# Down projections in 1024-column blocks, 9 of 22 pairs of k tiles by seven products, inner features in two sets, weight sums in place

## The chip, the cores and the metric

The kernel runs on one core of one Trainium2 chip. The metric is the device time of one execution in microseconds (us), the median of several runs. All arithmetic is float32. A product of float32 matrices is made from a rounded high part (`hi`, type fp32r) and a remainder (`lo`), as `x_hi*w_hi + x_hi*w_lo + x_lo*w_hi`: three matmuls of 128x128 by 128x512 for one product of a k tile.

## The reference, cut to what matters

Two layers; each is a mixer (retention and a gating unit in layer 0, a linear recurrence and sparse attention in layer 1) and then this feed-forward part, for 256 rows `x` of 2048 columns and 5632 inner features:

```
def swiglu(h, wg, wu, wd):
    return (jax.nn.silu(h @ wg) * (h @ wu)) @ wd
...
        h = rms_norm(x, ln_ffn_g[layer])
        x = x + swiglu(h, w_ffn_gate[layer], w_ffn_up[layer], w_ffn_down[layer]).astype(x.dtype)
```

The weights of the feed-forward parts are 264 of the loads of 1 MB of the kernel. The change touches only the feed-forward parts.

## The kernel before

**Units.** All weights come as loads of 1 MB into `raw` (three buffers), 128 partitions by 2048 numbers. In the feed-forward part a load is one *unit*. `ffn` makes the list of units in the order of the computation and issues each unit's preparation one unit ahead of its use (`AHEAD = 1`). The 5632 inner features are 11 groups of 512. Before, they go in three sets of 4, 4 and 3 groups: gate and up projections of the groups of a set (8 units for each group: a unit is two k tiles of 128 rows, gate and up columns side by side), then the down projection of that set, in four column blocks of 512 (`Down`; a unit is four k tiles).

**Plain units** (`"r"` in `KINDS`, made by `whole`). ScalarE rounds `raw` to `hi` in two halves of 1024 (`piece`, line 107), VectorE subtracts `lo = raw - hi` (line 108). TensorE makes 8 products, 24 matmuls. `hi` and `lo` have four buffers each (`HI`), so that a cast waits until TensorE is through with an earlier half.

**Seven-product units** (`"s"`, units 0, 3 and 6 of each group in `GateUp`). Seven products in the place of eight, 21 matmuls, after Winograd's form of Strassen's scheme: the two row halves of the activations and the four 128x512 blocks of the weights are combined by sums ahead of the products, and the seven results (PSUM banks `q1` to `q8`, without a number) are combined after them. `sums` makes the sums of the weights: three adds on VectorE (lines 300 to 302, 1024, 512 and 512 elements) from `raw` into a tile of their own, `sum`; `hi` and `lo` of the four sums (line 108 again); `hu` and `lu`, the two parts of three blocks as they came (lines 309 and 310, 1536 elements; one buffer each). `left` makes the sums of the activations. After the last seven-product unit of a group, `inner` takes four adds on VectorE out of PSUM; after the last unit of the group `outer` takes four more (line 371), a Silu (line 373) and a multiplication (line 374) for each half.

**Names in the texts.** M0, R1, R2, M3, R4, R5, M6, R7 are the units of a group: M for seven products, R for plain. The *boundary* of a group is R7, then the transposes of the results of an earlier group (`pt_hid`, 8 matmuls; `to_mix2`, put off in the list `late` and done at `flush`), then M0 and R1 of the next group.

**Order.** The order of the instructions on each engine isn't that of the code: a scheduler in the language places them, with the code's order as priority. Each engine works through its own list in that fixed order, and semaphores tie the engines together.

Of the kernel before, what the change touches and what calls it, by code (L numbers as in the profile page):

```python
# [31 lines left out]
KINDS = "srrsrrsr"  # L32
AHEAD = 1
FIRST = (1, 0, 2, 3, 4, 5, 6, 7)
MIXED = tuple(i for i, c in enumerate(KINDS) if c == "s")
# [5 lines left out]
def trunk(ctx: ExitStack, tc: tile.TileContext, d: dict, out: bass.AP):  # L41
# [18 lines left out]

    def T(shape, name, dt=F32):
        return now["T"].tile([128, *shape], dt, tag="T", name=name)
# [10 lines left out]
    def mix_tile(name):  # L73
        return act.tile([128, 2, 2, S], F32R, tag="B", name=name)
# [35 lines left out]

    def whole(src):

        raw = load(src, 2048)
        out = []
        for o in (0, 1024):
            hi, lo = piece(raw, o, 2, 512)
            out += [(hi[:, i, :], lo[:, i, :]) for i in range(2)]
        return out
# [105 lines left out]
    def left(src, gs):  # L224

        g, h = T([4, 128], "g"), T([4, 128], "h")
        nc.scalar.activation(g[:, 0:4:3, :], src[:, 0, :].rearrange("p (i n) -> p i n", i=2), AF.Copy, scale=gs[0])
        nc.scalar.activation(g[:, 1:3, :], src[:, 1, :].rearrange("p (i n) -> p i n", i=2), AF.Copy, scale=gs[1])
        nc.vector.tensor_sub(h[:, 0, :], g[:, 3, :], g[:, 2, :])
        nc.vector.tensor_sub(h[:, 3, :], g[:, 0, :], g[:, 3, :])  # L230
        nc.vector.tensor_sub(h[:, 1, :], h[:, 0, :], g[:, 0, :])
        nc.vector.tensor_add(h[:, 2, :], g[:, 1, :], h[:, 1, :])
        out = []
        for t, n in ((g, 3), (h, 4)):
            a = act.tile([128, 2, 4, 128], F32R, tag="A", name="A", bufs=8 + len(MIXED))
            nc.scalar.copy(a[:, 0, 0:n, :], t[:, 0:n, :])
            nc.vector.tensor_sub(a[:, 1, 0:n, :], t[:, 0:n, :], a[:, 0, 0:n, :].bitcast(F32))
            out += [(a[:, 0, i, :], a[:, 1, i, :]) for i in range(n)]
        return out

    class Norm:
# [8 lines left out]
        def operand(self, i, src):  # L250
            gs = [gain(self.g0 + 2 * i), gain(self.g0 + 2 * i + 1)]
            if i in self.mixed:
                self.tiles.append(left(src, gs))
# [60 lines left out]
    class GateUp:  # L314
# [4 lines left out]
        def __init__(self, n, hid, first):  # L319
            self.n, self.q, self.hid, self.first = n, {}, hid, first  # L320
            self.order = FIRST if first else range(8)

        def product(self, i, x2, hi, lo, last=False):
# [3 lines left out]
            (xh, xl), ps = x2, self.q[i]  # L327
# [4 lines left out]
        def use(self, i, w):  # L332
            j, end = self.order[i], i == 7
            if KINDS[j] != "s":
                a = self.n.tiles[j]
                for e, kt, cols in ((0, 0, ((2, 0), (4, 1))), (1, 1, ((2, 0), (4, 1))), (3, 0, ((3, 0), (8, 1))), (2, 1, ((3, 0), (8, 1)))):
                    for b, th in cols:
                        t = slice(128 * th, 128 * th + 128)
                        self.product(b, (a[:, kt, 0, t], a[:, kt, 1, t]), *w[e], end and e in (1, 2))
            else:  # L340
                a11, a12, a22, d1, d2, d3, d4 = self.n.tiles[j]
                s1, s2, s3, s4, b11, b21, b22 = w
                last = not any(k in MIXED for k in self.order[i + 1 :])
                self.product(5, d1, *s1, last)
                self.product(7, d4, *s2, last)
                self.product(6, d2, *s3, last)
                self.product(4, a22, *s4)
                self.product(1, a11, *b11, last)
                self.product(2, a12, *b21)
                self.product(3, d3, *b22)  # L350
                if last:
                    self.inner()
            if i == (0 if self.first else 7):
                flush()
            if end:
                self.outer()

        def inner(self):
            q = self.q
            c1, u2, u3, v, w = (T([512], n) for n in ("c1", "u2", "u3", "v", "w"))  # L360
            nc.scalar.copy(c1, q[1])
            nc.vector.tensor_add(u2, c1, q[6])
            nc.vector.tensor_add(u3, u2, q[7])
            nc.vector.tensor_sub(v, q[5], u2)
            nc.vector.tensor_sub(w, q[5], u3)
            self.c = {2: c1, 4: u3, 3: v, 8: w}

        def outer(self):
            c, n, s = self.c, self.n, []
            for i in (4, 2, 3, 8):  # L370
                nc.vector.tensor_add(c[i], self.q[i], c[i])
# [4 lines left out]
            late.append(partial(to_mix2, s, "hid", self.hid))  # L376

    class Down:


        def __init__(self, c, hid, total, done):
            self.c, self.hid, self.total, self.done = c, hid, total, done

        def use(self, i, w):
            xs = pairs(self.hid)
            if i == 0:
                self.ps = two(512, "pd")
            end = i == self.total - 1
            order = [(j, th) for th in range(2) for j in range(4)] if end else [(j, th) for j in range(4) for th in range(2)]
            for j, th in order:  # L390
                xh, xl = xs(4 * i + j)
                t = slice(128 * th, 128 * th + 128)
                hi, lo = w[j]
                mm(self.ps[th], xh[:, t], hi, start=i + j == 0, stop=False)  # L394
                mm(self.ps[th], xh[:, t], lo, start=False, stop=False)  # L395
                mm(self.ps[th], xl[:, t], hi, start=False, stop=end and j == 3)  # L396
            if i == 0:
                flush()
            if end:
                add_x(self.c, self.ps)  # L400
                self.done(self.c)

    def ffn(layer, n, norm):
        wgu, wd = d[f"wgu{layer}"], d[f"wd{layer}"]
        f = stage(f"f{layer}", TF)
        fp = f.enter_context(tc.tile_pool(name=f"sums{layer}", bufs=1))

# [8 lines left out]
        for g0, gn in ((0, 4), (4, 4), (8, 3)):  # L416
            hid = []
            for g in range(g0, g0 + gn):
                gu = GateUp(n, hid, g == 0)
                units += [(wgu[g, j], KINDS[j], partial(gu.use, i)) for i, j in enumerate(gu.order)]  # L420
            for c in range(4):
                dn = Down(c, hid, gn, done if g0 == 8 else lambda c: None)
                units += [(wd[c, g0 + i], "r", partial(dn.use, i)) for i in range(gn)]
        ready = {}
        for i, (_, _, use) in enumerate(units):
            for k in range(i, min(i + AHEAD + 1, len(units))):
                src, kind, _ = units[k]
                if k not in ready:
                    ready[k] = sums(src, fp) if kind == "s" else whole(src)
# [14 lines left out]
    lp = c0.enter_context(tc.tile_pool(name="l0", bufs=1))  # L444
    lng = lp.tile([128, 2, 512], F32, name="lng")
# [167 lines left out]
    lp = c1.enter_context(tc.tile_pool(name="l1", bufs=1))  # L613
    masks = lp.tile([128, 7, 128], I32, name="masks")
# [355 lines left out]
def _gate_up(g, u):  # L970

    g, u = (w.reshape(8, 2, 128, -1, 512).transpose(3, 0, 2, 1, 4) for w in (g, u))
    return np.ascontiguousarray(np.stack([g[:, :, :, 0], g[:, :, :, 1], u[:, :, :, 1], u[:, :, :, 0]], 3)).reshape(-1, 8, 128, 2048)
# [33 lines left out]
def _layout(i):  # L1007
# [11 lines left out]
    for l in range(2):  # L1019
        o[f"wgu{l}"] = _gate_up(i["w_ffn_gate"][l], i["w_ffn_up"][l])  # L1020
        o[f"wd{l}"] = _wide(i["w_ffn_down"][l], 512)
# [29 lines left out]
```

## Time and profile before

| | before |
|---|---|
| median of 3 runs | 2218.31 us (2217.01 to 2219.98) |
| the profiled execution: its time | 2217.86 us |
| its span, first to last instruction | 2216.1 us |
| TensorE matmuls (PE) | 10199, busy 2203.8 us |
| TensorE weight loads (PEld) | busy 1830.6 us |
| VectorE (DVE) | busy 1622.4 us |
| ScalarE (ACT) | busy 1121.1 us |
| GpSimd (POOL) | busy 12.1 us |
| mean granted TensorE clock | 1.000 |

Busy times overlap, since the engines work side by side. Matmuls are pipelined and the ends of their records are modelled, so the time that a matmul costs in a full stream is read from the distance of the starts.

### The profile page before, as it was taken

Reading aid. Unit: us, or ns where it says so; the run is one execution under the profiler, and the core shown is the slowest. Engines: PE = TensorE matmul, PEld = TensorE weight load, DVE = VectorE, ACT = ScalarE, POOL = GpSimd, SP = SyncE. Lnnn points to the kernel's source line nnn. Section 1 sums busy time; section 2 is a strip of 40 time slices with the busy share of each in tenths; the row PEclk is TensorE's granted clock in tenths of the full one; section 3 lists DMA queues with packets and bytes.
Section 4 is the critical chain, followed back from the end, with each engine's and each line's share of the span. In section 5 each row is a group of like instructions: output and inputs, shape, how many; then the busy total and the mean of one; then the engine's idle time right before and its main releaser. Section 6 shows DMA issues by size and latency. Waiting matters only on the chain.

```text
span 2216.1 us, 26309 instructions
## 1 busy us (share of the span) xinstructions
PE 2203.8 (99%) x10199; PEld 1830.6 (83%) x10199; DVE 1622.4 (73%) x2227; ACT 1121.1 (51%) x1368; POOL 12.1 (1%) x24
## 2 busy tenths in 40 slices
PE   9999999999999999999999999999999999999999
PEld 7888878888888888888888888888888888888887
DVE  6745657988568975797655788869886688857884
ACT  6444435655445553555555355556554455534543
POOL 0000000000000000000000000000000000000000
PEclk9999999999999999999999999999999999999999
DMA  8555465555555555555455443354555555555554
GB/s 330 199 189 198 156 162 209 190 206 195 186 192 209 190 190 193 205 186 208 165 198 189 148 152 114 133 180 186 209 209 179 207 200 191 191 191 209 188 192 152
DMA packets 63437, 419.67 MB, mean 189 GB/s; under 512 B 7672, under 2 KB 7672, under 8 KB 15696
## 3 DMA queue, kind: packets, MB, share of 16 engines
q1 hardware_dynamic: 60704, 412.51, 51.0%
q0 software_dynamic: 1312, 3.33, 0.8%
q10 hardware_dynamic: 1296, 2.15, 0.3%
q8 instruction: 80, 1.31, 0.2%
q14 instruction: 45, 0.37, 0.0%
HBM read 414.29 MB, written 3.67 MB: 189 GB/s over the span
## 4 chain that ended last, share of the span: by engine, by line
PE 97%; DVE 1%; DMA 1%; ACT 0%; issue 0%; SPq 0%; ACTq 0%
PE q L328 14%; PE q L329 14%; PE q L330 14%; PE pd L396 7%; PE pd L395 7%; PE pd L394 7%; PE po L161 2%; PE po L162 2%; PE po L160 2%; PE pqk L161 1%; PE pqk L162 1%; PE pqk L160 1%; PE plv L818 1%; DMA raw<-in_ev_out 1%; PE pt_hid L201 1%; PE pvs L160 1%
## 5 line engine op out<-in xcount | busy, mean ns | idle before, releaser
L108 DVE TENSOR_TENSOR lo<-raw,hi 128x1024 fp32r<-128x1024 f32 (+3 forms) x652 | 780.2, 1207 | 457.6 <-ACT hi L107 454.5
L107 ACT CAST hi<-raw 128x1024 fp32r<-128x1024 f32 (+3 forms) x652 | 674.5, 1039 | 737.7 <-PE pd L396 216.7
L328 PE MATMUL q<-hi,A 128*128 128x512 f32 x1144 | 446.7, 390 | 0.0
L329 PE MATMUL q<-lo,A 128*128 128x512 f32 x1144 | 446.0, 390 | 0.0
L330 PE MATMUL q<-hi,A 128*128 128x512 f32 x1144 | 445.2, 389 | 0.0
L394 PE MATMUL pd<-hi,hid 128*128 128x512 f32 x704 | 275.2, 391 | 0.0
L396 PE MATMUL pd<-hi,hid 128*128 128x512 f32 x704 | 274.0, 389 | 0.0
L395 PE MATMUL pd<-lo,hid 128*128 128x512 f32 x704 | 274.0, 389 | 0.0
L328 PEld LDWEIGHTS q<-hi,A 128*128 128x128 f32 x1144 | 214.8, 188 | 45.5
L330 PEld LDWEIGHTS q<-hi,A 128*128 128x128 f32 x1144 | 214.8, 188 | 45.3
L329 PEld LDWEIGHTS q<-lo,A 128*128 128x128 f32 x1144 | 214.8, 188 | 44.9
L107 ACT CAST hi<-sum 128x1024 fp32r<-128x1024 f32 x132 | 138.6, 1050 | 189.9 <-PE q L330 81.7
L108 DVE TENSOR_TENSOR lo<-sum,hi 128x1024 fp32r<-128x1024 f32 x132 | 161.6, 1224 | 68.4 <-ACT hi L107 64.7
L396 PEld LDWEIGHTS pd<-hi,hid 128*128 128x128 f32 x704 | 132.1, 188 | 27.5
L395 PEld LDWEIGHTS pd<-lo,hid 128*128 128x128 f32 x704 | 132.2, 188 | 27.0
L394 PEld LDWEIGHTS pd<-hi,hid 128*128 128x128 f32 x704 | 132.2, 188 | 27.0
L309 ACT CAST hu<-raw 128x1536 fp32r<-128x1536 f32 x66 | 97.7, 1480 | 56.9 <-PE q L330 40.0
L310 DVE TENSOR_TENSOR lu<-raw,hu 128x1536 fp32r<-128x1536 f32 x66 | 115.7, 1753 | 3.7 <-ACT hu L309 3.6
L300 DVE TENSOR_TENSOR sum<-raw 128x1024 f32<-128x1024 f32 x66 | 80.6, 1221 | 3.3 <-DMA raw<-in_wgu 2.7
L328 PE MATMUL q<-hu,A 128*128 128x512 f32 x198 | 78.4, 396 | 0.2
L330 PE MATMUL q<-hu,A 128*128 128x512 f32 x198 | 78.4, 396 | 0.0
L329 PE MATMUL q<-lu,A 128*128 128x512 f32 x198 | 77.7, 392 | 0.0
(379 smaller groups left out, 3026.4 us busy)
## 6 DMA issues: line engine op xcount, KB each, us to landing
raw<-in_wgu SPq DMA_DIRECT2D x176, 1024.0 KB, 4.8
raw<-in_wd SPq DMA_DIRECT2D x88, 1024.0 KB, 4.8
raw<-in_ev_in SPq DMA_DIRECT2D x44, 1024.0 KB, 4.8
raw<-in_od_in SPq DMA_DIRECT2D x32, 1024.0 KB, 4.8
raw<-in_ev_out SPq DMA_DIRECT2D x16, 1024.0 KB, 4.8
raw<-in_od_out SPq DMA_DIRECT2D x16, 1024.0 KB, 4.7
raw<-in_od_z SPq DMA_DIRECT2D x8, 720.0 KB, 4.0
raw<-in_ev_in SPq DMA_DIRECT2D x6, 512.0 KB, 7.4
```

Of the source, the lines that this page charges most:

```text
L107: nc.scalar.copy(hi[:, :e], raw[:, o : o + e])
L108: nc.vector.tensor_sub(lo[:, :e], raw[:, o : o + e], hi[:, :e].bitcast(F32))
L160: mm(ps[th], xh[:, c], hi[:, j, :], start=i + j == 0, stop=False)
L300: nc.vector.tensor_add(sm[:, 0:2, :], r[:, 0:3:2, :], r[:, 3:4, :].to_broadcast([128, 2, 512]))
L309: nc.scalar.copy(hu, r[:, 0:3, :])
L310: nc.vector.tensor_sub(lu, r[:, 0:3, :], hu.bitcast(F32))
L328: mm(ps, xh, hi, start=first, stop=False)
L329: mm(ps, xh, lo, start=False, stop=False)
L330: mm(ps, xl, hi, start=False, stop=last)
L394: mm(self.ps[th], xh[:, t], hi, start=i + j == 0, stop=False)
L395: mm(self.ps[th], xh[:, t], lo, start=False, stop=False)
L396: mm(self.ps[th], xl[:, t], hi, start=False, stop=end and j == 3)
```

## The change

It makes a single class `Block` for the gate/up groups and for the down projection. The inner features go in two sets, of 6 and 5 groups. The down projection of a set goes in two column blocks of 1024 (`cp` 0 and 1), 12 or 10 units each; a unit is one pair of k tiles with the four 128x512 blocks of the weights, as in a gate/up unit. Of the pairs 1, 3, 5, 7, 9 (first set) and 1, 3, 5, 7 (second set) the products are seven, in both column blocks. So these pairs' activations `hid` are made by `left` (sums of the row halves), where the others keep `split`. In the second column block each seven-product unit stands ahead of the plain one before it. The results are added to `x` straight from the PSUM banks (`grow`), half of them after the last seven-product unit and half after the last unit.

`right` takes the place of `whole` and `sums`: it makes `hu` and `lu` first, then sums the blocks of weights in place in `raw`, then `hi` and `lo` of the sums. The tile `sum` is gone, and the room goes to 17 buffers for `hid` in the place of 8. The order of the products in a seven-product unit is now 1 (with `hu`), 5, 7, 6 (sums), 2, 3 (`hu`), 4 (a sum) in the code; before it was 5, 7, 6, 4 (sums), then 1, 2, 3 (`hu`).

```diff
-KINDS = "srrsrrsr"
-AHEAD = 1
+SETS = ((0, 6), (6, 5))
+MIXED = (0, 3, 6)
...
+HIDDEN = {6: (1, 3, 5, 7, 9), 5: (1, 3, 5, 7)}
...
-    def sums(src, fp):
+    def right(src, mixed, pool):
...
         raw = load(src, 2048)
-        r = raw.rearrange("p (i n) -> p i n", i=4)
-        sm = fp.tile([128, 4, 512], F32, tag="sum", name="sum")
-        nc.vector.tensor_add(sm[:, 0:2, :], r[:, 0:3:2, :], r[:, 3:4, :].to_broadcast([128, 2, 512]))
-        nc.vector.tensor_add(sm[:, 2, :], sm[:, 0, :], r[:, 2, :])
-        nc.vector.tensor_add(sm[:, 3, :], sm[:, 2, :], r[:, 1, :])
         parts = []
-        for i in range(2):
-            hi, lo = piece(sm.rearrange("p i n -> p (i n)"), 1024 * i, 2, 512)
-            parts += [(hi[:, e, :], lo[:, e, :]) for e in range(2)]
-        hu = fp.tile([128, 3, 512], F32R, tag="hu", name="hu")
-        lu = fp.tile([128, 3, 512], F32R, tag="lu", name="lu")
-        nc.scalar.copy(hu, r[:, 0:3, :])
-        nc.vector.tensor_sub(lu, r[:, 0:3, :], hu.bitcast(F32))
-        parts += [(hu[:, i, :], lu[:, i, :]) for i in range(3)]
+        if mixed:
+            r = raw.rearrange("p (i n) -> p i n", i=4)
+            hu = pool.tile([128, 3, 512], F32R, tag="hu", name="hu")
+            lu = pool.tile([128, 3, 512], F32R, tag="lu", name="lu")
+            nc.scalar.copy(hu, r[:, 0:3, :])
+            nc.vector.tensor_sub(lu, r[:, 0:3, :], hu.bitcast(F32))
+            parts += [(hu[:, i, :], lu[:, i, :]) for i in range(3)]
+            nc.vector.tensor_add(r[:, 0:4:3, :], r[:, 0:3:2, :], r[:, 3:4, :].to_broadcast([128, 2, 512]))
+            nc.vector.tensor_add(r[:, 2, :], r[:, 0, :], r[:, 2, :])
+            nc.vector.tensor_add(r[:, 1, :], r[:, 2, :], r[:, 1, :])
+        for o in (1024, 0):
+            hi, lo = piece(raw, o, 2, 512)
+            parts += [(hi[:, i, :], lo[:, i, :]) for i in range(2)]
         return parts
...
+            if j in self.mixed:
+                a11, a12, a22, d1, d2, d3, d4 = a
+                b11, b21, b22, s3, s2, s1, s4 = w
+                last = not any(k in self.mixed for k in self.order[i + 1 :])
+                self.product(1, a11, b11, last)
+                self.product(5, d1, s1, last)
+                self.product(7, d4, s2, last)
+                self.product(6, d2, s3, last)
+                self.product(2, a12, b21)
+                self.product(3, d3, b22)
+                self.product(4, a22, s4)
+                if last:
+                    self.inner(self.q)
...
+            def keep():
+                for i in range(2):
+                    src = turn([t[:, 256 * i : 256 * i + 256] for t in s], "pt_hid")
+                    if flags[i]:
+                        hid.append(left(src, (1.0, 1.0), lambda: mix_tile("hid").rearrange("p a b (c n) -> p a (b c) n", n=128)))
+                    else:
+                        m = mix_tile("hid")
+                        split(m, src)
+                        hid.append(m)
...
+    def down(w, cp, hid, mixed, n, done):
+        def grow(q):
+            for i, (th, e) in ((2, (0, 0)), (3, (0, 1)), (4, (1, 0)), (8, (1, 1))):
+                xs = x[2 * cp + e][:, th, :]
+                nc.vector.tensor_add(xs, q[i], xs)
...
+        order = list(range(n))
+        if cp:
+            for j in mixed:
+                order[j - 1], order[j] = j, j - 1
+        return Block(w, hid, order, mixed, n - 1 if cp else 0, lambda q: grow(inner_sums(q)), outer).units()
...
-        for g0, gn in ((0, 4), (4, 4), (8, 3)):
+        for g0, gn in SETS:
```

What it does to the lists of the engines is seen best at the boundary of a group. The first place is VectorE's list in layer 0, from the sums of the next group's M0 on. Before (`u`, `v`, `w`, `c` are the partial sums of the finished group, `lo<-sum` belongs to a seven-product unit, `lo<-raw` to a plain one):

```order
L300 TENSOR_TENSOR sum<-raw 128x1024
L301 TENSOR_TENSOR sum<-sum,raw 128x512
L108 TENSOR_TENSOR lo<-raw,hi 128x1024
L302 TENSOR_TENSOR sum<-sum,raw 128x512
L108 TENSOR_TENSOR lo<-raw,hi 128x1024
L108 TENSOR_TENSOR lo<-sum,hi 128x1024 x2
L362 TENSOR_TENSOR u_5504<-c_5503,q_5268 128x512
L363 TENSOR_TENSOR u_5505<-u_5504,q_5264 128x512
L364 TENSOR_TENSOR v<-q_5260,u_5504 128x512
L365 TENSOR_TENSOR w<-q_5260,u_5505 128x512
L310 TENSOR_TENSOR lu<-raw,hu 128x1536
```

And of the change, the same boundary between the inner adds of a group (which stand just ahead of these rows) and the first `lo` of R1 (seven rows stand between these and it); L299 is `lu`, L301 to L303 are the sums, L372 are the outer adds, L202 and L223 to L225 make `hid`:

```order
L299 TENSOR_TENSOR lu<-raw,hu 128x1536
L372 TENSOR_TENSOR v<-q_4418,v 128x512
L301 TENSOR_TENSOR raw<-raw 128x2x512
L372 TENSOR_TENSOR w<-q_4439,w 128x512
L302 TENSOR_TENSOR raw<-raw 128x512
L372 TENSOR_TENSOR c_4639<-q_4414,c_4639 128x512
L303 TENSOR_TENSOR raw<-raw 128x512
L111 TENSOR_TENSOR lo<-raw,hi 128x1024
L202 TENSOR_TENSOR hid<-pt_hid,hid 128x2x256
L111 TENSOR_TENSOR lo<-raw,hi 128x1024
L223 TENSOR_TENSOR h<-g 128x128
L224 TENSOR_TENSOR h<-g 128x128
```

The three sums and the two `lo` of M0 stood ahead of the inner adds and now stand behind them, and `lu` of M0 is ahead of its sums in the place of behind them.

The second place is ScalarE's list at the same boundaries. Before, from the inner copy `c` on (`hu` is M0's, `hi<-raw` are those of R1 and R2):

```order
L361 COPY c_5503<-q_5276 128x512
L309 CAST hu<-raw 128x1536
L107 CAST hi<-raw 128x1024
L373 ACTIVATE u_5505<-u_5505,r 128x512
L207 CAST hid<-pt_hid 128x2x256 x2
L373 ACTIVATE c_5503<-c_5503,r 128x512
L107 CAST hi<-raw 128x1024 x3
```

And of the change (the first two `hi` are M0's, the two in one row are R1's; `g` and `h` are the tiles of `left`, L374 is the Silu):

```order
L359 COPY c_4639<-q_4398 128x512
L298 CAST hu<-raw 128x1536
L110 CAST hi<-raw 128x1024
L201 CAST hid<-pt_hid 128x2x256
L110 CAST hi<-raw 128x1024
L221 ACTIVATE g<-pt_hid 128x2x128
L222 ACTIVATE g<-pt_hid 128x256
L374 ACTIVATE c_4639<-c_4639,r 128x512
L230 CAST hid<-g 128x384
L110 CAST hi<-raw 128x1024 x2
L230 CAST hid<-h 128x512
L374 ACTIVATE u_4641<-u_4641,r 128x512
```

Both `hi` of M0, which before stood ahead of the copy, now stand behind it, and the work of `left` stands between them and the rest.

The third place is TensorE's list at the same boundary of the change, from the end of M0 into R1 (lines 326, 327 and 328 are the three matmuls of a product; `q_4755`, `q_4751`, `q_4776` and `q_4759` are the banks of R1):

```order
L327 MATMUL q_4759<-lo,A 128x512
L328 MATMUL q_4759<-hi,A 128x512
L326 MATMUL q_4755<-hi,A 128x512
L326 MATMUL q_4751<-hi,A 128x512
L326 MATMUL q_4776<-hi,A 128x512
L326 MATMUL q_4759<-hi,A 128x512
L327 MATMUL q_4755<-lo,A 128x512
L328 MATMUL q_4755<-hi,A 128x512
```

In the rows of before every product's three matmuls stand together (`hi`, `lo`, `hi`, as in the down projection):

```order
L394 MATMUL pd_4363<-hi,hid 128x512
L395 MATMUL pd_4363<-lo,hid 128x512
L396 MATMUL pd_4363<-hi,hid 128x512
L394 MATMUL pd_4364<-hi,hid 128x512
L395 MATMUL pd_4364<-lo,hid 128x512
L396 MATMUL pd_4364<-hi,hid 128x512
```

In the change, four matmuls with `hi` of R1 stand ahead of the first that needs its `lo`.

## Rows read from the trace of the kernel before

**Rows 1.** Page, part 1: busy us (share of the span) and instructions.

```profile
PE 2203.8 (99%) x10199; PEld 1830.6 (83%) x10199; DVE 1622.4 (73%) x2227; ACT 1121.1 (51%) x1368; POOL 12.1 (1%) x24
```

**Rows 2.** Waits of PE, the longest: us in total, times, longest us.

```profile
PE po L160 <- ACT hi L107: 2.7, 1, 2.7
```

**Rows 3.** Windows, a group and a down projection: us; PE, PEld, DVE, ACT busy.

```profile
509.27:557.35 48.08, 48.08 (x217) 39.63 (x215) 41.54 (x46) 26.05 (x27) 0.00 (x0) 1.00 0.58 214
558.10:646.20 88.10, 88.10 (x396) 73.04 (x395) 50.20 (x50) 36.56 (x37) 0.00 (x0) 1.00 0.53 191
```

**Rows 4.** Timeline of PE (start us, us), down projection, two starts 24 matmuls apart.

```profile
640.06 0.39 PE L394 MATMUL pd<-hi,hid 128*128 128x512 f32 x1
...
645.50 0.39 PE L394 MATMUL pd<-hi,hid 128*128 128x512 f32 x1
```

**Rows 5.** Timeline of PE at a boundary: starts of M6, R7, transposes, M0, R1.

```profile
504.45 0.39 PE L328 MATMUL q<-hi,A 128*128 128x512 f32 x1
...
509.27 0.39 PE L328 MATMUL q<-hi,A 128*128 128x512 f32 x1
...
514.74 0.27 PE L201 MATMUL pt_hid<-ident,c 128*128 128x128 f32 x1
...
515.53 0.48 PE L328 MATMUL q<-hi,A 128*128 128x512 f32 x1
...
520.44 0.39 PE L328 MATMUL q<-hi,A 128*128 128x512 f32 x1
520.67 0.40 PE L329 MATMUL q<-lo,A 128*128 128x512 f32 x1
```

**Rows 6.** Timeline of DVE at the same boundary.

```profile
504.60 0.68 DVE L302 TENSOR_TENSOR sum<-sum,raw 128x512 f32<-128x512 f32 x1
...
509.64 0.68 DVE L362 TENSOR_TENSOR u<-c,q 128x512 f32<-128x512 f32 x1
...
512.16 1.75 DVE L310 TENSOR_TENSOR lu<-raw,hu 128x1536 fp32r<-128x1536 f32 x1
513.83 0.69 DVE L371 TENSOR_TENSOR u<-q,u 128x512 f32<-128x512 f32 x1
514.43 0.68 DVE L371 TENSOR_TENSOR c<-q,c 128x512 f32<-128x512 f32 x1
...
518.45 0.75 DVE L374 SCALAR_TENSOR_TENSOR u<-w,r,u 128x512 f32<-128x512 f32 x1
519.12 4.63 DVE L108 TENSOR_TENSOR lo<-raw,hi 128x1024 fp32r<-128x1024 f32 x4
```

**Rows 7.** Groups by form, ACT: count, busy us, mean ns, idle before.

```profile
L107 ACT CAST hi<-raw 128x1024 fp32r<-128x1024 f32 x624 | 653.5, 1052 | 713.3 <-PE pd L396 214.2 <-PE q L330 169.4 <-PE po L162 63.9
...
L309 ACT CAST hu<-raw 128x1536 fp32r<-128x1536 f32 x66 | 97.7, 1480 | 56.9 <-PE q L330 40.0 <-DMA raw<-in_wgu 9.6 <-ACT hi L107 7.2
...
L207 ACT CAST hid<-pt_hid 128x512 fp32r<-128x512 f32 x44 | 23.6, 588 | 1.0
...
L373 ACT ACTIVATE c<-c,r 128x512 f32<-128x512 f32 x22 | 16.0, 725 | 0.0
```

**Rows 8.** Tiles of `left` (g, h): ns min/median/max, first and last start.

```profile
L227 ACT ACTIVATE g<-pxt,gains x6: 465/466/470, 358.6 to 1509.1; 128x256 f32<-128x256 f32 x6
...
L236 ACT CAST A<-g x6: 513/514/515, 359.4 to 1510.0; 128x384 fp32r<-128x384 f32 x6
L229 DVE TENSOR_TENSOR h<-g x6: 282/284/289, 359.8 to 1510.4; 128x128 f32<-128x128 f32 x6
...
L237 DVE TENSOR_TENSOR A<-g,A x6: 551/552/555, 360.4 to 1511.0; 128x384 fp32r<-128x384 f32 x6
...
L237 DVE TENSOR_TENSOR A<-h,A x6: 683/692/692, 361.9 to 1514.0; 128x512 fp32r<-128x512 f32 x6
```

**Rows 9.** Timeline of PE soon after the start, two neighbours.

```profile
8.42 0.63 PE L161 MATMUL pvs<-lo,A 128*128 128x512 f32 x1
8.84 0.63 PE L162 MATMUL pvs<-hi,A 128*128 128x512 f32 x1
```

More of the change, by code (lines that the diff above doesn't have):

```diff
@@ new lines, in right, with __init__, units, product @@
+        for o in (1024, 0):
+            hi, lo = piece(raw, o, 2, 512)
+            parts += [(hi[:, i, :], lo[:, i, :]) for i in range(2)]
+        return parts
+    class Block:
+        def __init__(self, w, a, order, mixed, flush_at, inner, outer):
+            self.w, self.a, self.order, self.mixed, self.flush_at, self.inner, self.outer = w, a, order, mixed, flush_at, inner, outer
+            self.q = {}
+        def units(self):
+            return [(self.w[j], j in self.mixed, partial(self.use, i)) for i, j in enumerate(self.order)]
+        def product(self, i, x2, w2, last=False):
@@ L332, in use @@
         def use(self, i, w):
[L333 to L337, printed above, removed]
-                        t = slice(128 * th, 128 * th + 128)
[L339 to L352, printed above, removed]
@@ L353, in use @@
-            if i == (0 if self.first else 7):
+            j, end = self.order[i], i == len(self.order) - 1
+            a = self.a[j]
+            if j in self.mixed:
[12 more added lines that the diff above has]
+            else:
+                for e, kt, cols in ((0, 1, (3, 8)), (1, 0, (3, 8)), (2, 0, (2, 4)), (3, 1, (2, 4))):
+                    for th in range(2):
+                        t = slice(128 * th, 128 * th + 128)
+                        self.product(cols[th], (a[:, kt, 0, t], a[:, kt, 1, t]), w[e], end and e in (1, 3))
@@ L354, in use @@
+            if i == self.flush_at:
                 flush()
             if end:
[L356 to L366, printed above, removed]
@@ L372, in outer, with gate_up @@
+    def gate_up(w, n, hid, flags, first):
+        c = {}
+        def outer(q):
+            s = []
+            for i in (2, 3, 4, 8):
+                nc.vector.tensor_add(c[i], q[i], c[i])
             for th, (g, u) in enumerate(((2, 3), (4, 8))):
@@ L375, in outer @@
                 s.append(c[g])
[L376 to L401, printed above, removed]
+            def keep():
[3 more added lines that the diff above has]
+                        hid.append(left(src, (1.0, 1.0), lambda: mix_tile("hid").rearrange("p a b (c n) -> p a (b c) n", n=128)))
+                    else:
+                        m = mix_tile("hid")
+                        split(m, src)
+                        hid.append(m)
+            late.append(keep)
+        return Block(w, n.tiles, FIRST if first else range(8), n.mixed, 0 if first else 7,
+                     lambda q: c.update(inner_sums(q)), outer).units()
+    def down(w, cp, hid, mixed, n, done):
[3 more added lines that the diff above has]
+                nc.vector.tensor_add(xs, q[i], xs)
+        def outer(q):
+            grow(q)
+            for e in range(2):
+                done(2 * cp + e)
+        order = list(range(n))
[3 more added lines that the diff above has]
+        return Block(w, hid, order, mixed, n - 1 if cp else 0, lambda q: grow(inner_sums(q)), outer).units()
     def ffn(layer, n, norm):
@@ L415, in ffn @@
         units = []
-        for g0, gn in ((0, 4), (4, 4), (8, 3)):
-            hid = []
+        for g0, gn in SETS:
+            hid, mixed = [], HIDDEN[gn]
             for g in range(g0, g0 + gn):
[L419 to L424, printed above, removed]
+                i = 2 * (g - g0)
+                units += gate_up(wgu[g], n, hid, (i in mixed, i + 1 in mixed), g == 0)
+            for cp in range(2):
+                units += down(wd[cp, 2 * g0 :], cp, hid, mixed, 2 * gn, done if g0 else lambda c: None)
+        ready = []
         for i, (_, _, use) in enumerate(units):
[L426 to L429, printed above, removed]
+            while len(ready) < min(i + 2, len(units)):
+                ready.append(right(*units[len(ready)][:2], fp))
             use(ready[i])
```

53 lines of the change are left out of this document (26 added, 27 removed).

## Prediction, made blind

> **What bounds the kernel now.** I read the page's busy times first: matmuls fill 99% of the span, no other engine more than 73% [rows 1]. Then PE's own waits: the longest of the whole execution is 2.7 us, once, outside the feed-forward part [rows 2]. So every unit's weights arrive in time, and the time is the number of matmuls times their distance. In the down projection 24 starts take 645.50 - 640.06 = 5.44 us, 0.2267 us each [rows 4]. A seven-product unit (M6, 504.45 to 509.27) takes 4.82 us for 21: twelve at 0.2267, the nine with `hu` and `lu` 0.233 [rows 5]. The cover is uneven, though: VectorE is busy 41.54 of 48.08 us of a group (86%), 50.20 of 88.10 in the down projection (57%) [rows 3]. The change loads both.
>
> [...] The trace has the starts evenly 0.2267 us apart without a wait, so the distance decides.
>
> **What is removed.** 9 pairs x 2 column blocks x 2 layers = 36 units lose one product each: 108 matmuls x 0.2267 = 24.5 us. Their nine matmuls with `hu` go from 0.2267 to 0.233: 36 x 9 x 0.0067 = 2.2 us back. Net **-22.3 us**, if no weight comes late. The bytes and the number of loads stay.
>
> **What is added, at the boundary of a group.** I lay the change's lists against the clock there, with time 0 at the start of R7.
>
> Before: VectorE has done M0's three sums by 505.28, 4 us ahead of R7 (509.27), in idle time; then inner adds, `lu`, outer adds, `hid`, and R1's `lo` at 519.12, at 9.85 [rows 6]. TensorE comes to R1 at 520.44 and to its first `lo` at 520.67 [rows 5]; that `lo` ended at about 520.34. The slack is 0.3 us.
>
> In the change the sums overwrite `raw`, so they wait for `lu`, `lu` for `hu`, and `hu` (one buffer) for M6's last product with it, about 0.5 us ahead of time 0. Everything for M0 then falls into R7 and M0. Durations: back to back, a `lo` or the sum of 1024 costs VectorE 1.14 (a quarter of 4.63 less the tail), an add of 512 0.60 (513.83 to 514.43), `lu` 1.67, the last multiplication 0.67 [rows 6]; `hi` 1.05, `hu` 1.48, `hid` 0.59, Silu 0.72 [rows 7]; the steps of `left` 0.47, 0.51, 0.28, 0.55, 0.69 [rows 8] (back to back about 0.09 less each).
> - VectorE: inner adds early, -2.0 to 0.45, since M6 now makes products 1, 5, 7, 6 first. `hu` is ready at 1.03; `lu` to 2.73; three outer adds and three sums in turn to 6.87 (3 x 0.60 + 1.14 + 2 x 0.60).
> - ScalarE: first `hi` of M0 from the second sum, 5.86 to 6.91; `hid` to 7.45; second `hi` to 8.5; two of `g` to 9.25; Silu 9.87; cast of `g` 10.3; both `hi` of R1 to 12.2; only then the cast of `h`, 12.75; Silu 13.38.
> - VectorE: `lo` of M0 6.95 to 8.1, `hid` 8.7, `lo` 9.9; three of `h`, `hid` from `g` 11.0; one of `h`, outer add, multiplication 12.4; `hid` from `h` waits for its cast, 12.8 to 13.4; the multiplication that needs the second Silu 14.07; then R1's `lo`, ready at **15.3**.
> - TensorE: R7 and transposes to 6.26 (515.53 - 509.27 [rows 5]); M0's nine `hu` matmuls to 8.35; 0.2 for the second `hi`, some waits of a tenth, M0 out at 11.57 where 11.08 is due; four matmuls with R1's `hi`, the second `hi` 0.5 late, to 12.95; then **2.4 us** for R1's `lo`. The other 20 end at 15.33 + 20 x 0.2267 = 19.86.
> Without waits R1 ends at 6.26 + 4.82 + 5.44 = 16.52. So a boundary loses **3.35 us**. Behind VectorE's list at that point stand R2's `lo` and M3's `lu`; they end 0.5 to 2 us ahead of TensorE again, because TensorE is late itself, so the loss isn't passed on, nor made good.
>
> There are 14 boundaries with all of this (4 in the first set, 3 in the second, two layers): 14 x 3.35 = 46.9 us.
>
> No row of before shows this wait, so bounds. Below: with no `hid` to make (the first boundary of a set) the same reckoning gives 1.25 us, 17.5 in all. Above: none of the early start, that is what VectorE has more ahead of R1's `lo` (sums 2.34, two `lo` 2.28, `left` 1.3) less the slack: 5.6 us, 78 in all. I take 3.35, since each of its steps has a row. A gain at the boundary is excluded: PE doesn't wait there now.
>
> **The other places**, reckoned in the same way:
> - 4 boundaries without `hid`: 1.25 each, 5.0.
> - 4 times from the last group into the down projection: VectorE has two groups' `hid` in R7 and the first plain unit, M's `hi` comes 0.9 late: 1.1 each, 4.4.
> - 4 times between the column blocks: eight adds (inner 4, `x` 4, 4.8 us) ahead of a plain unit's `lo`, four more between the next unit's sums, and the cast of the next-but-one `hu` ahead of the second `hi`: 2.75 each, 11.0.
> - Pairs M and R in the down projection: from `hu` to the release of `hu` the chain is `hu` 1.48, `lu` 1.67, the first two sums 1.9, `hi` 1.05, two `lo` 2.4, then 4 to 6 matmuls to the last with `hu`, 1.1 to 1.5, and I allow 0.4 for semaphores (an estimate): 10.0 to 10.4 us, against 4.82 + 5.44 = 10.26 of TensorE. At most 0.15 each: 3.
> - From the first set's down projection into the next group, twice: 2.
> Together 25.4. The end is as before: one add and a transfer behind the last matmul.
>
> **Sum**: -22.3 + 46.9 + 25.4 = +50.0 us. The profiled execution took 2217.86 us (span 2216.1 and 1.8 around it), 0.5 below the median of 2218.31; so 2217.9 + 50 = **2268 us**.
>
> **The rivals.**
> 1. *VectorE makes it in time.* The 22.3 us come in full, some 3 us of small waits stay: 2199. For it: in a whole group VectorE has 14% idle [rows 3], and the added work (1.3 us of `left` a group) would fit into it. Against it: the idle time lies in R2 to R5, and in-place sums can't be made there for M0. It is faster than before as long as all waits together stay under 22.3 us, 0.7 a place over the 30 places; R1's `lo` would have to be there at 12.5, not 15.3. 20 in 100.
> 2. *Half of it.* VectorE recovers where ScalarE doesn't hold it, and a full boundary loses what one without `hid` does: 17.5 + 25.4 - 22.3 = +20.6, 2238; with the other places lower still it ends at no change. 18 in 100, of which 6 within 0.2%.
> 3. *The down pairs are bound by the chain.* If each step takes a tenth longer, a pair loses 0.5 more: 36 x 0.5 = 18, 2286. The row for it is VectorE's idle time behind `hu`; against it, the durations of one form differ by less than 3% [rows 8]. 5 in 100.
> 4. *TensorE slows after each wait.* Near the start, neighbours are 0.42 us apart [rows 9], and 0.2267 later. If ten matmuls behind each of the 14 waits ran so, that were 14 x 10 x 0.2 = 28 us more: 2296. Against it: the page grants the full clock, 1.00, in both windows [rows 3], and the waits reckoned are shorter than the one of 2.7 us that is there already [rows 2]. 5 in 100. [...]
> My forecast (2250 to 2280) has the other 52.
>
> **How the numbers follow.** About 0.2% is what a measurement can tell from no change here. Faster by more: rival 1, 20 in 100. Within: 6. Slower: the forecast, the rest of rival 2, rivals 3 and 4, 74. The range leaves out most of rival 1 and the upper end of rival 4: 2206 to 2292; the likeliest case's own is 2250 to 2285.
>
> **What the profile will show.** Right: PE's waits name R1's `lo` (line 111 of the changed kernel) some 14 times at 2 to 3 us and `hi` (line 110) at most of the 30 places; 108 matmuls fewer; distances of 0.2267 between the waits; VectorE without idle time from `lu` of M0 to R2's `lo`. Wrong: PE without waits of over 0.5 us (then rival 1), waits that recur inside the down pairs (rival 3), distances of 0.4 us (rival 4). The forecast fails if VectorE gets to R1's `lo` much before 14 us behind R7's start, by steps that overlap more than these rows let me see.

## The result, and the profile after

The changed kernel takes **2296.82 us** (median of 4 runs, 2293.43 to 2297.30), the kernel before 2218.49 in the same comparison: a ratio of 1.035 (95% interval 1.0332 to 1.0368), 78 us slower. The forecast of 2268 us had the direction and missed the size; the time lies 5 us above the range. The profiled execution took 2297.12 us, with a span of 2295.3, 79.2 more than the span before.

The page of the changed kernel, part 1 (busy us, share of the span, instructions), beside [rows 1]:

```profile
PE 2237.3 (97%) x10091; PEld 1817.9 (79%) x10091; DVE 1828.7 (80%) x2509; ACT 1166.1 (51%) x1466; POOL 12.1 (1%) x24
```

TensorE has the 108 matmuls fewer that were announced, and is nevertheless busy 33.5 us longer: matmuls cost more each. VectorE has 206 us more work. TensorE's waits (us in total, times, longest us), beside [rows 2]:

```profile
PE q L327 <- DVE lo L111: 29.4, 14, 2.1
PE q L326 <- ACT hi L110: 10.5, 12, 2.2
PE q L326 <- ACT hu L298: 4.8, 3, 1.6
```

The first is the wait that the prediction named, at R1's `lo`, 14 times. The boundary of the third and the fourth group of layer 0, in the timeline of PE (start, us):

```profile
518.90 0.39 PE L326 MATMUL q<-hi,A 128*128 128x512 f32 x1
...
525.13 0.48 PE L326 MATMUL q<-hu,A 128*128 128x512 f32 x1
525.45 0.39 PE L327 MATMUL q<-lu,A 128*128 128x512 f32 x1
525.68 0.40 PE L328 MATMUL q<-hu,A 128*128 128x512 f32 x1
...
527.08 0.40 PE L328 MATMUL q<-hu,A 128*128 128x512 f32 x1
...
530.24 1.45 PE L326 MATMUL q<-hi,A 128*128 128x512 f32 x4
533.79 0.50 PE L327 MATMUL q<-lo,A 128*128 128x512 f32 x1 [2.10 <-DVE lo L111]
...
536.13 0.63 PE L327 MATMUL q<-lo,A 128*128 128x512 f32 x1
536.56 0.63 PE L328 MATMUL q<-hi,A 128*128 128x512 f32 x1
...
538.69 0.40 PE L326 MATMUL q<-hi,A 128*128 128x512 f32 x1
538.92 0.40 PE L327 MATMUL q<-lo,A 128*128 128x512 f32 x1
```

R7 starts at 518.90, M0 at 525.13, R1 at 530.24 (11.34 behind R7's start; reckoned 11.57), its first matmul with `lo` at 533.79 (14.89; reckoned 15.33). VectorE at the same place:

```profile
519.95 1.76 DVE L299 TENSOR_TENSOR lu<-raw,hu 128x1536 fp32r<-128x1536 f32 x1 [0.27 <-ACT hu L298]
521.63 0.69 DVE L372 TENSOR_TENSOR v<-q,v 128x512 f32<-128x512 f32 x1
...
531.85 0.75 DVE L375 SCALAR_TENSOR_TENSOR u<-w,r,u 128x512 f32<-128x512 f32 x1
532.52 4.62 DVE L111 TENSOR_TENSOR lo<-raw,hi 128x1024 fp32r<-128x1024 f32 x4
```

Between `lu` of M0 and R1's `lo` it has no idle time. Both lists ran as reckoned. What had not been reckoned stands behind the wait. From 535.3 to 538.7 the starts are 0.427 us apart (536.13 to 536.56), before and after 0.23. The windows of the same stretch (us; then busy time and count of PE, PEld, DVE, ACT and POOL; then the granted clock, the DMA share and GB/s):

```profile
518.90:530.24 11.34, 11.34 (x54) 9.12 (x53) 11.07 (x18) 6.53 (x10) 0.00 (x0) 1.00 0.22 77
535.30:538.65 3.35, 3.35 (x9) 2.62 (x8) 3.35 (x3) 0.00 (x0) 0.00 (x0) 0.50 0.66 252
538.70:545.51 6.81, 6.81 (x32) 5.63 (x30) 6.22 (x7) 3.06 (x3) 0.00 (x0) 1.00 0.51 191
```

The granted clock is 0.50 there, and 1.00 in the windows around it. The feed-forward parts have 14 such stretches (10 of the 14 boundaries, 3 of the 4 places between column blocks, 1 boundary without `hid`), before they had none. A fifteenth, at 330.5 us, lies ahead of them, behind a wait that the kernel before has as well. A second thing stands in the down projection, away from every wait; the plain unit of pair 6 in the first column block, its first start and that of the next unit, 24 matmuls on:

```profile
698.34 0.39 PE L326 MATMUL q<-hi,hid 128*128 128x512 f32 x1
...
703.91 0.39 PE L326 MATMUL q<-hu,hid 128*128 128x512 f32 x1
```

5.57 us, 0.232 each, where [rows 4] have 5.44 and 0.2267, without a wait and at full clock.

**Where the 79.2 us are.** I added over all matmuls of 512 columns of either trace the distance to the next start less 0.2267, apart for starts in stretches at the lower clock, for other distances above 0.27 (waits), and for the rest by the tiles that are read:

| us, after less before | measured | reckoned |
|---|---|---|
| 108 matmuls fewer | -24.5 | -24.5 |
| waits | +64.8 | +72.3 |
| stretches at the lower clock: feed-forward parts 21.4, the one ahead of them 1.5 | +22.9 | 0 (rival 4: 28) |
| distances without a wait: `hid` 10.1, mixers' tiles 4.1, rest 1.8 | +16.0 | +2.2 |
| sum | +79.2 | +50.0 |

The mixers' tiles (`mixa` to `mixh`, the operands of the output projections) are in no row of the prediction: the change moves their buffers, with `hid`'s, out of the pool `act` into pools of their own. Their 768 matmuls go from 0.2275 to 0.233 us on the mean.

### The profile page after: what moved, and what is told of

It is laid out like the page before. It is cut to its first block, busy times and chain, and to the rows that moved or that the text cites. A ratio compares the mean times of both kernels' runs of the same rounds, so it can differ in the third digit from the quotient of the medians.

```text
span 2295.3 us, 26470 instructions
## 1 busy us (share of the span) xinstructions
PE 2237.3 (97%) x10091; PEld 1817.9 (79%) x10091; DVE 1828.7 (80%) x2509; ACT 1166.1 (51%) x1466; POOL 12.1 (1%) x24
## 4 chain that ended last, share of the span: by engine, by line
PE 83%; DVE 9%; issue 4%; ACT 3%; DMA 1%; SPq 0%; ACTq 0%
PE q L327 17%; PE q L328 17%; PE q L326 17%; DVE lo L111 3%; PE po L155 2%; PE po L156 2%; PE po L154 2%; ACT hu L298 1%; PE pqk L156 1%; PE pqk L155 1%; PE pqk L154 1%; PE plv L825 1%; ACT hi L110 1%; DMA raw<-in_ev_out 1%; DVE raw L301 1%
## 5 line engine op out<-in xcount | busy, mean ns | idle before, releaser
L110 ACT CAST hi<-raw 128x1024 fp32r<-128x1024 f32 (+3 forms) x784 | 792.8, 1040 | 927.8 <-DVE raw L302 422.0
L111 DVE TENSOR_TENSOR lo<-raw,hi 128x1024 fp32r<-128x1024 f32 (+3 forms) x784 | 923.6, 1209 | 357.7 <-ACT hi L110 356.8
L327 PE MATMUL q<-lo,hid 128*128 128x512 f32 x560 | 223.7, 400 | 0.0
L328 PE MATMUL q<-hi,hid 128*128 128x512 f32 x560 | 222.1, 397 | 0.0
L326 PE MATMUL q<-hi,hid 128*128 128x512 f32 x560 | 213.8, 405 | 4.5 <-ACT hi L110 4.5
L299 DVE TENSOR_TENSOR lu<-raw,hu 128x1536 fp32r<-128x1536 f32 x102 | 179.2, 1757 | 43.4 <-ACT hu L298 40.4
L298 ACT CAST hu<-raw 128x1536 fp32r<-128x1536 f32 x102 | 150.7, 1477 | 96.6 <-issue 64.7
L326 PEld LDWEIGHTS q<-hi,hid 128*128 128x128 f32 x560 | 106.5, 191 | 36.4 <-ACT hi L110 12.9
L327 PEld LDWEIGHTS q<-lo,hid 128*128 128x128 f32 x560 | 106.1, 190 | 29.1 <-DVE lo L111 0.7
L301 DVE TENSOR_TENSOR raw<-raw 128x1024 f32<-128x1024 f32 x102 | 124.7, 1223 | 2.3
L328 PEld LDWEIGHTS q<-hi,hid 128*128 128x128 f32 x560 | 106.1, 189 | 23.3
L302 DVE TENSOR_TENSOR raw<-raw 128x512 f32<-128x512 f32 x102 | 70.4, 690 | 2.6
L303 DVE TENSOR_TENSOR raw<-raw 128x512 f32<-128x512 f32 x102 | 70.3, 689 | 2.4
```

The lines of the kernel that those rows point to most:

```text
L110: nc.scalar.copy(hi[:, :e], raw[:, o : o + e])
L111: nc.vector.tensor_sub(lo[:, :e], raw[:, o : o + e], hi[:, :e].bitcast(F32))
L301: nc.vector.tensor_add(r[:, 0:4:3, :], r[:, 0:3:2, :], r[:, 3:4, :].to_broadcast([128, 2, 512]))
L302: nc.vector.tensor_add(r[:, 2, :], r[:, 0, :], r[:, 2, :])
L303: nc.vector.tensor_add(r[:, 1, :], r[:, 2, :], r[:, 1, :])
L326: mm(ps, xh, hi, start=first, stop=False)
```

## The experiments

All times are medians, with the kernel before in the same runs (2218.0 to 2218.8).

**1. Where the tiles stand.** In the program of before, `hid` and the mixers' tiles begin at multiples of 1024 bytes of a partition; in the changed one `hid`, `hu` and `lu` begin 640 bytes past one, `mixa` and `mixb` 672, `mixd` and `mixh` 832. Unused pads put them back:

```diff
+    rp.tile([128, 96], F32, tag="pad", name="pad", bufs=1)
     dp = ctx.enter_context(
...
+    lp.tile([128, 248], F32, name="pad0")
     mixed_operands(c0, "m0", 8)
...
+    lp.tile([128, 208], F32, name="pad1")
     mixed_operands(c1, "m1", 8)
```

> The changed kernel with three unused pads (384, 992 and 832 bytes a partition), so that the tiles hid, mixa, mixb, mixd, mixh, hu and lu begin at multiples of 1024 bytes as before, and nothing else. Theory (the place of a tile in the memory sets the distance of the matmuls that read it): the distance of matmuls with hid and with the four mix tiles falls from 0.232 us to 0.2267, that of those with hu and lu too; 14 us with hid and mix, 3 more with hu and lu: about 2280 us (2277 to 2285). Rival (the distance is longer because VectorE and ScalarE work more at the same time): distances stay, 2297, within 3.

Measured: **2282.07 us**, 14.8 less. The same unit as above:

```profile
697.59 0.39 PE L327 MATMUL q<-hi,hid 128*128 128x512 f32 x1
...
703.03 0.39 PE L327 MATMUL q<-hu,hid 128*128 128x512 f32 x1
```

5.44 us. Summed as above, the matmuls with `hid` lost 8.7 us of their excess, the mixers' 4.2, those with `hu` and `lu` in the gate projections 2.5. Waits took some of it back (5 us more of them), and two stretches at the lower clock fewer gave 3.5. VectorE's busy time is the same (1827.4 us), so its work is not what made the matmuls slower; the rival fell. The operand that stood badly was the stationary one with `hid` and the moving one with `hu`; either cost 0.005 to 0.006 us a matmul.

**2. The same in the kernel before.** There only `hu` and `lu` begin 640 bytes past a multiple (the 0.233 of [rows 5]). The first of the three pads alone:

> The kernel before with one unused pad of 384 bytes a partition, so that sum, hu and lu begin at multiples of 1024 bytes; hid and the mix tiles begin there already. Theory (a tile's place sets the distance, for the moving operand as for the stationary one): the 594 matmuls with hu and lu go from 0.233 to 0.2267 us: 2218.3 - 3.7 = 2214.6 us (2212.5 to 2216.5). Rival (the 0.233 belongs to something else that these matmuls share, as the order of the products): 2218, within 1.5.

Measured: **2214.70 us**, ratio 0.9981 (0.9972 to 0.9990). Nine matmuls of a seven-product unit with `hu` and `lu`, the first start and the last:

```profile
508.62 0.39 PE L329 MATMUL q<-hu,A 128*128 128x512 f32 x1
...
510.43 0.39 PE L331 MATMUL q<-hu,A 128*128 128x512 f32 x1
```

1.81 us for eight distances, 0.2263. The 0.233, which the prediction had read as belonging to `hu`, belonged to its place. Half of the slices of the activations `A` begin 512 bytes past a multiple of 1024, and they ran at 0.2267 throughout.

**3. The clock.** Nine matmuls more at each of the 14 boundaries (R1's first matmul of bank 8, made again and again with `start=True`, ahead of the real one):

```diff
+                if i == 1 and self.fill:
+                    self.f8 = PM([512], "q8")
+                    for _ in range(self.fill):
+                        mm(self.f8, a[:, 1, 0, 128:256], w[0][0], start=True, stop=True)
...
-                units += gate_up(wgu[g], n, hid, (i in mixed, i + 1 in mixed), g == 0)
+                units += gate_up(wgu[g], n, hid, (i in mixed, i + 1 in mixed), g == 0, 9 if g - g0 >= 2 else 0)
```

> The changed kernel with nine extra matmuls (a first product of R1 made nine times over and then again as it should be; the result is unchanged) between the last matmul that R1 can make with hi and the first that needs its lo, at the 14 boundaries where TensorE waits there; 9 x 0.2267 = 2.04 us of work inside a wait of some 2.3 us. Theory (the wait lowers the clock, and the slow matmuls behind it are lost time of their own): the granted clock stays at 1.00 at these boundaries and the matmuls behind stay 0.2267 apart; ten or eleven boundaries give 1.6 us back each: about 2280 us (2277 to 2284). Rival (the matmuls behind the wait are slow because their operands come late): no change, 2297, or some us more.

Measured: **2277.56 us**, 19.3 less, with 126 matmuls more. R1 of the same boundary, from its first `lo` on:

```profile
531.07:537.00 5.93, 5.93 (x26) 4.89 (x27) 5.89 (x5) 1.39 (x1) 0.00 (x0) 1.00 0.60 224
```

Clock 1.00, distances 0.23; none of the 14 boundaries has a stretch at the lower clock. Two of the four other stretches are gone too, where nothing was filled in; such stretches come and go between executions (the mean clock of the kernel before is 0.998 to 1.000, execution by execution). Matmuls that compute nothing new made this kernel 19.3 us faster: with them in the wait the granted clock stayed at 1.00, without them it was 0.50 behind 10 of the 14 waits. So the low clock followed from the wait here and was a price of its own: eight matmuls at 0.427, 1.6 us.

**4. Without the sums in place.**

```diff
+            sm = pool.tile([128, 4, 512], F32, tag="sum", name="sum")
+            nc.vector.tensor_add(sm[:, 0:4:3, :], r[:, 0:3:2, :], r[:, 3:4, :].to_broadcast([128, 2, 512]))
...
             hu = pool.tile([128, 3, 512], F32R, tag="hu", name="hu")
...
-            nc.vector.tensor_add(r[:, 0:4:3, :], r[:, 0:3:2, :], r[:, 3:4, :].to_broadcast([128, 2, 512]))
...
-                self.product(1, a11, b11, last)
                 self.product(5, d1, s1, last)
                 self.product(7, d4, s2, last)
                 self.product(6, d2, s3, last)
+                self.product(4, a22, s4)
+                self.product(1, a11, b11, last)
...
-HIDDEN = {6: (1, 3, 5, 7, 9), 5: (1, 3, 5, 7)}
+HIDDEN = {6: (1, 3, 5), 5: (1, 3, 5, 7)}
```

> The changed kernel with the sums of the weights in a tile of their own, ahead of hu and lu, and the products in the order of before (5, 7, 6, 4, then 1, 2, 3). The tile takes 8 KB a partition, so two pairs fewer of the first set go by seven products (1, 3, 5 in the place of 1, 3, 5, 7, 9; 8 units, 24 matmuls, 5.4 us more). Theory (it is the sums in place that put the preparation of M0 behind R7's start): the waits at all 18 boundaries and the slow clock behind them go, some 43 + 9 + 20 us; 2297 - 72 + 5 = 2230 us (2220 to 2238). Rival (the activations' sums for hid, made at the boundary, keep VectorE late by themselves): the waits at R1's lo stay at 1 to 2 us, 2260 or more.

Measured: **2229.29 us**, 67.5 less than the changed kernel. Its longest waits of PE in the feed-forward part:

```profile
PE q L333 <- DVE lo L111: 5.2, 12, 0.4
```

The boundaries without `hid` lose nothing any more, the places between column blocks 0.4 us, the 14 boundaries 12.4 us together (43.0 in the changed kernel, the clock apart). The order of the products goes back together with the sums, so this run doesn't tell the two apart; the two pairs fewer cost 24 matmuls, 5.4 us.

**5. The sums in place alone,** in the kernel before (the sums of `sums` into `raw`, `hu` and `lu` first, the product order of the change; no other edit):

> The kernel before with one part of the change alone: hu and lu first, then the sums in place in the load, the products in the order of the change; down projection, sets and hid as before. Theory (the sums in place make the wait at the boundary; the activations' sums only lengthen it): waits of 1.3 to 2.5 us at the 20 boundaries, some of them with a slow clock behind: 2218 + 25 to 55, about 2255 us. Rival (without the new down projection VectorE has time enough): 2218, within 5.

Measured: **2245.82 us**, ratio 1.0122 (1.0105 to 1.0139), 27 us slower, at the low end of what I expected; 16 of the 20 boundaries lose 1.3 to 1.7 us each, the four behind a down projection nothing. There is no stretch at the lower clock in the feed-forward parts. PE's waits:

```profile
PE q L328 <- DVE lo L108: 11.7, 16, 1.0
PE q L327 <- ACT hi L107: 2.7, 6, 0.5
```

**6. The work of `left` away from the boundary.** The copies out of PSUM stay, the rest goes behind the fourth unit of the next group:

```diff
         nc.scalar.activation(g[:, 1:3, :], src[:, 1, :].rearrange("p (i n) -> p i n", i=2), AF.Copy, scale=gs[1])
+        out = []
+
+        def rest():
+            left_rest(g, h, tile, out)
...
+            defer.append(rest)
+        return out
+
+    def left_rest(g, h, tile, out):
         nc.vector.tensor_sub(h[:, 0, :], g[:, 3, :], g[:, 2, :])
...
+            if i == 3:
+                while late3:
+                    late3.pop(0)()
```

> The changed kernel with the work of left in two: the two copies out of PSUM into g stay at the boundary, the sums h and the casts and subtractions of hid from g and h are issued three units later, behind the fourth unit of the next group. Theory (at a boundary the sums in place cost what they cost in e4_before_in_place, 27 us for 20 boundaries, 1.35 each, and the steps of left the rest of the 3.07): 14 x 1.7 = 24 us less, and some 12 less of the slow clock: 2261 us (2250 to 2275). Rival (the chain hu, lu, sums, hi, lo alone sets R1's lo, and the steps of left lie in its gaps): 2290 or more.

Measured: **2240.22 us**, 57 less than the changed kernel, with the sums still in place. My estimate was too high by 21 us: the wait at R1's `lo` isn't among PE's waits any more.

```profile
PE q L338 <- ACT hi L110: 8.3, 8, 2.2
PE q L338 <- ACT hu L310: 4.8, 3, 1.6
```

The 14 boundaries lose 6.5 us together and have no stretch at the lower clock. So the boundary's loss is not a sum of a part for the sums in place and a part for `left`: it is 0.5 us with the sums in place here, 0.9 with `left` in experiment 4, 0.3 with neither (the second last kernel of experiment 8) and 3.1 with both. VectorE's list there has some slack; either load alone stays near it, both together pass it by over 2 us, and the clock is 0.50 behind 10 of the 14. Why the same sums cost 1.3 to 1.7 us a boundary in the kernel before (experiment 5), with other work around them, isn't shown.

**7. `hu` free earlier.**

```diff
                 self.product(1, a11, b11, last)
+                self.product(2, a12, b21)
+                self.product(3, d3, b22)
                 self.product(5, d1, s1, last)
                 self.product(7, d4, s2, last)
                 self.product(6, d2, s3, last)
-                self.product(2, a12, b21)
-                self.product(3, d3, b22)
```

> The changed kernel with one thing else: the products of a seven-product unit in the order 1, 2, 3 (with hu and lu), then 5, 7, 6 and 4 (with the sums). The sums stay in place. Theory (the preparation of M0 is late because hu, one buffer, is held until M6 is nearly over): hu is free some 2 us earlier, the wait at R1's lo falls from 2.1 us to below 0.6, with less of the slow clock behind it: 2297 - 14 x 1.7 - 10 = 2263 us (2245 to 2275). Rival (the inner adds, now 1.3 us later, take VectorE's place again, and the list is as long as before): 2290 to 2300.

Measured: **2298.07 us**, no change; the rival was right. `lu` of M0 starts 1.0 us ahead of R7 in the place of 1.05 behind, yet R1's `lo` comes at the same time, since all four inner adds now lie behind R7's start, where three lay ahead of it. R7's start and that `lo`, of this kernel:

```profile
518.45 0.39 PE L326 MATMUL q<-hi,A 128*128 128x512 f32 x1
...
532.48 4.62 DVE L111 TENSOR_TENSOR lo<-raw,hi 128x1024 fp32r<-128x1024 f32 x4
```

14.03 us, against 13.62 (518.90 to 532.52). At these boundaries it was the length of the list that counted, not when its head might start. The unchanged total hides moves at other places: between the column blocks the waits fall from 9.5 to 1.1 us and in the pairs from 3.7 to nothing, but into the down projection they rise from 4.0 to 14.5, and at the 14 boundaries from 43.0 to 48.8.

**8. Towards a faster kernel.** Own sums and pads:

> Own sums (as in e3_own_sums: a tile for the sums, the old order of products, two pairs fewer) and the three pads of e1_align together. Theory (the two causes are independent): the 14.7 us that the pads gave in e1_align come off again, and with hu and lu included 15 to 18: 2229.3 - 16 = 2213 us (2209 to 2216), faster than before. Rival (a shorter distance only makes the weights late, because VectorE is as busy as TensorE here): waits at lo grow by what the distance gives, 2222 or more.

Measured: **2213.59 us**, ratio 0.9980 (0.9971 to 0.9989). That is just what the pad alone gives the kernel before: the down projection by seven products, 19 us of matmuls, is used up by the boundaries (13.1 us) and smaller waits. Then with three sets and every second pair by seven products, the seven-product unit first or second in a block (`SETS = ((0, 4), (4, 4), (8, 3))`, `HIDDEN = {4: (0, 2, 4, 6), 3: (0, 2, 4)}`):

> Own sums, the old order of products, the pads, and the inner features in three sets of 4, 4 and 3 groups again, which needs 12 tiles for hid in the place of 17 and leaves room for the sums' tile: the even pairs go by seven products (0, 2, 4, 6 of eight, 0, 2, 4 of six; 11 of 22 in the place of 7 of 22 in f1_own_sums_align; 132 matmuls fewer than before). Theory: 48 matmuls x 0.2267 = 10.9 us under f1_own_sums_align, 2 to 3 less for four boundaries with fewer sums of activations, 2 to 4 more for the third set's adds into x: 2202 us (2198 to 2208). Rival (every pair by seven products in turn makes VectorE the bound in the down projection): waits within the pairs, 2212 or more.

Measured: **2258.36 us**, a miss by 56. The rival's time is nearer, its place wrong: within the pairs there is next to nothing; the losses are at the edges of the column blocks, where a seven-product unit now stands directly behind the eight adds of the block before (3 to 5 us at each step from the first block to the second, with the lower clock behind some).

```profile
PE q L333 <- ACT hi L111: 28.8, 22, 4.8
PE q L333 <- DVE hid L203: 6.9, 16, 0.8
```

Own sums, pads and the later `left`:

> Own sums, the old order of products, the pads (f1_own_sums_align), and the work of left in two as in f7_defer. Theory (the 0.5 at R1's lo and the 0.3 at the matmuls with hi behind the boundary are VectorE and ScalarE with left; 11 boundaries lose 1.07 each): 2213.6 - 11 = 2202.5 us (2199 to 2207), faster than both kernels. Rival (the sums of left in the middle of a group make R4's or R5's lo late there): 2211 or more.

Measured: **2204.01 us**, ratio 0.9935 (0.9922 to 0.9949). And with one pair more:

> The same with eight pairs in the place of seven (1, 3, 5, 7 of the first set's twelve), for which one tile more of hid is paid by two buffers fewer of the small tiles T (8 in the place of 10). Theory: 12 matmuls x 0.2267 = 2.7 us under f8_own_sums_align_defer, 2200 us. Rival (T's buffers are needed: g waits for the results of the last group): not below f8_own_sums_align_defer, some us above.

Measured: **2200.37 us**, ratio 0.9922 (0.9910 to 0.9934): 18 us below the kernel before, 96 below the changed one. Its longest waits of PE:

```profile
PE po L157 <- ACT hi L111: 3.2, 1, 3.2
PE pw L94 <- POOL idle L91: 2.5, 1, 2.5
PE q L345 <- ACT hi L111: 1.0, 2, 0.5
```

The first two lie outside the feed-forward parts.

## Why the prediction was right or wrong, point by point

**Removed: 24.5 us.** Right: 10091 matmuls.

**Waits at the boundaries: 46.9 reckoned, 43.0 measured.** Right in place, number and mechanism: R1's first `lo` matmul at 14.89 us behind R7's start against 15.33, 3.07 a boundary against 3.35. Experiments 4, 5 and 6 show that it takes both the sums in place and `left` at this place.

**Other places: 25.4 reckoned.** Boundaries without `hid` 5.0, measured 7.7; into the down projection 4.4, measured 4.0; between column blocks 11.0, measured 9.5; pairs 3, measured 3.7; from the first set into the next group 2, measured 0. (With 1.1 in the first groups that is 69.1 us; the feed-forward parts of before have 3.1 of such waits, and the waits outside them fell by 1.1, hence the 64.8 of the table.) Right within 1.5 us each but for the first and the last. The 2.7 us in the first place are a step that was left out. Two of these four boundaries lose 1.3 us, as reckoned, the other two, the first of each layer, 2.5 and 2.6: there ScalarE loads a table ahead of the first Silu, between the two `hi` of M0.

```profile
433.34 1.05 ACT L110 CAST hi<-raw 128x1024 fp32r<-128x1024 f32 x1 [4.81 <-DVE raw L302]
434.41 1.28 ACT L374 ACT_TABLE_LOAD   x1
```

The kernel before has the same load, 1.28 us at 431.66, but behind both `hi` of M0, where it cost nothing. The 0.4 us that the chain of a pair allows for semaphores had no row in the prediction, and no run shows it; at the boundary above, `lu` starts 0.03 us behind the end of `hu` (518.44 + 1.48, then 519.95).

**Distances: "distances of 0.2267 between the waits" and "2.2 us back". Wrong, the first failed step.** It took the distance of the matmuls with `hid` from a kernel in which `hid` stood elsewhere. The move into a pool of its own cost 14.2 us over the 2772 matmuls with `hid` and the mixers' tiles, 0.005 each on the mean. Reckoned +2.2, measured +16.0; pads take 14.8 off (experiment 1).

**The clock: rival 4 at 5 in 100. Wrong, the second failed step.** It was set against the forecast, though it could only come on top of it. The argument against it, one longer wait in the trace before with no loss of clock behind it, rested on one execution. At the same wait (`po`, `hi` of an output projection) the clock falls in 11 of the 13 traces; before and experiment 7 are the other two. In the trace of experiment 2, the kernel before with one pad, the wait and the stretch behind it are:

```profile
PE po L161 <- ACT hi L108: 2.9, 1, 2.9
```

```profile
331.60:334.99 3.39, 3.39 (x10) 2.61 (x9) 3.28 (x5) 1.15 (x2) 0.00 (x0) 0.50 0.75 239
```

The price was set too high: a stretch cost 1.5 to 1.6 us where 2.0 were reckoned, and 10 of the 14 boundaries have one, 15.2 us in the place of 28; 6.2 more came at other places of the feed-forward parts. That rival 4's time, 2296, is the measured one is chance: against the forecast the waits were 7.5 us less, the distances 13.8 more and the clock 22.9 more, together 29 where the rival has 28. The runs show a granted clock of 0.50 behind 10 of 14 boundaries, where waits of 2.1 us were enough, and 1.00 behind all of them once the wait is filled (experiment 3). Why 4 of 14 waits of the same length kept the clock, the traces don't show.

**Rivals 1 and 2** (VectorE in time, or half) fell with the waits. **Rival 3** (down pairs bound by the chain): 3.7 us of waits in 28 units are not the 18 of the rival.

With the two failed terms put right, -24.5 + 16.0 + 22.9 and the 72.3 of waits as reckoned would have given +86.7, 2305 us.

## What to carry to other kernels

A wait reckoned on TensorE may have to be paid twice. Here 14 boundaries cost 43.0 us of waits, and the matmuls behind 10 of them, at a granted clock of 0.50, 15.2 us more; with nine matmuls in each wait that change nothing, the clock stayed at 1.00 behind all 14, and the run took 19.3 us less. A change that moves buffers into another pool can move addresses: look up where each operand of TensorE begins before and after, and try pads; those to multiples of 1024 bytes took 14.8 us off the changed kernel. Where a list of an engine was full at one place of the schedule, what helped here was to make it shorter there (sums in a tile of their own ahead of time, with the order of products of before, 67.5 us less; work put off into a stretch with idle time, 57 us less), not to let its head start earlier (no change). And a row that shows one execution doesn't show that a thing cannot happen: look for the same place in other executions.

## What the runs showed of the hardware that was not expected

- A matmul of 128x128 by 128x512 took 0.2267 us from start to start where both operands began at a multiple of 512 bytes, 0.232 to 0.233 where the stationary one (640, 672 or 832 bytes past a multiple of 1024) or the moving one (640) did not. Where neither did (`hu` and `lu` with `hid`) it was 0.230 to 0.232, no more than with one. Other offsets were not tried.
- Waits of TensorE of 2.1 us with a few matmuls around them brought the granted clock to 0.50 for about eight matmuls (0.427 us apart) behind 10 of 14 boundaries. A wait of 1.3 to 3.4 us for `po`, the same one in all kernels, with one of 0.5 to 0.8 behind it, did so in 11 of 13 traces. In the kernels whose waits in the feed-forward parts stay at or below 1.0 us there was none of it there (experiments 4 and 5, and in 8 all but the one with three sets).
